# Modulation products queued in whole blocks, and recurrent states stored as transposed rows

## Chip, cores and metric

One core of a Trainium2 chip runs the whole kernel. The metric is device time in microseconds (us) of one execution, as the median of several.

## The reference, cut to what matters

Two layers of a trunk run for 128 context tokens and 512 latent tokens together. What the change touches is the modulation vector of each layer and the final state of the recurrence:

```python
for l in range(DEPTH):                                   # DEPTH = 2, D_MODEL = 1024
    mod_ctx = (jax.nn.silu(c_ctx) @ ada_w[l] + ada_b[l])[None, None, :]   # 6 * 1024 values
    y_p, (st, nk, nv, dk, dv) = trunk_layer(y_p, mod_ctx, context_mixer, p)
    mod_lat = (jax.nn.silu(c) @ ada_w[l] + ada_b[l])[:, None, :]
    y_s, _ = trunk_layer(y_s, mod_lat, latent_mixer, p)
...
sh_a, sc_a, g_a, sh_f, sc_f, g_f = jnp.split(mod, 6, axis=-1)   # shift, scale, gate of both halves of a layer
...
hf = linear_scan(af, bf, h0f, False); hb = linear_scan(ab, bb, h0b, True)
return y, hf[:, -1], hb[:, 0]        # st: 2 directions x 512 values per layer, an output of the kernel
```

## The kernel before, in words

Both token groups are kept as 640 columns, with the features on the partitions. A layer is a mixer (recurrence, neighbourhood attention, differential attention, out projection) and a feed-forward network. Large products split each operand into a high and a low part and do three products for one (L265 to L267, L274 to L276, L1235 to L1237). Loads, TensorE products, splits on ScalarE (L110) and VectorE (L117), and everything else are written as one program; a scheduler orders each engine's instructions by priority, where an instruction written earlier goes first as soon as its inputs stand. The helper `later(n)` shifts that priority by n for what is written inside it.

**Modulation.** A group of 2048 of the 6144 modulation values is one generator `ada_group`. It takes eight steps. A step loads 1 MB of `ada_w` into a raw tile (L195, tile `adaw`) and issues four products (L204, tile `ada`), one for each 32-row strip of the accumulator, all with the same 32-column stationary operand `cT[:, k]` and 512 columns of weights each. Five such groups run (40 steps, 160 products, each of which shows as two records in the trace): two in the mixer of each layer and one, for layer 1, in the feed-forward network of layer 0. Who calls the generator advances it with `next(ada)` after a part of its own work, so a step stands between other products. Nothing ties a step's four products together: the scheduler may put others between them. The first 1024-column pieces of layer 0 are done ahead in `ada_first` in the same manner with 128 columns each.

**Raw tiles.** The pool `rawp` has two tiles. Weights of the in projection (`w`), `ffn_up` (`up`) and `ada_w` share them, so a load waits until a tile's reader is done. All DMAs stand in one queue, SyncE's (SP), in order.

**States.** The scan of block j writes the last value of each direction into column `nstate[:, l, dr, j]` (L705): 128 features on the partitions. After the mixer the program stores them (L1456) with one DMA for each direction, 128 partitions by 4 columns, which goes to DRAM as 512 pieces of 4 bytes. Its inputs stand early, so the scheduler puts both stores of a layer into the SP queue in the middle of the neighbourhood attention.

Of the kernel before, what the change touches and what calls it, by code (L numbers as in the profile page):

```python
# [2 lines left out]

# [1 line left out]

# [12 lines left out]
P = 128  # L18
D = 1024
KD = D // P  # L20
# [48 lines left out]
def trunk_kernel(ctx: ExitStack, tc: tile.TileContext, A, O):  # L69
    nc = tc.nc  # L70
# [123 lines left out]
    def ada_load(l, g, k, w):  # L194
        nc.sync.dma_start(w, dram(A["ada_w"], (l * D + k * P) * 6144 + g * 2048, ((6144, P), (1, 2048))))  # L195
        return w

    def ada_group(l, g):
        acc = ps_a.tile([P, 512], F32, tag="ada", name="ada")
        for k in range(KD):  # L200
            w = ada_load(l, g, k, raw_tile("adaw"))
            with later(50 if l and g == 0 else 0):
                for q in range(4):
                    nc.tensor.matmul(acc[32 * q:32 * q + 32], cT[:, k], w[:, q * 512:q * 512 + 512],  # L204
                                     start=(k == 0), stop=(k == KD - 1))
            yield
        row = g_tile(512, name="adar")
        copy("a", row, acc)
        pt = s_tile()
        for u in range(4):  # L210
            nc.tensor.transpose(pt[:, u * P:u * P + P], row[:, u * P:u * P + P], ident)
        o = mod[l][:, g * 16:g * 16 + 16, :]
        for s in range(2):
            nc.vector.tensor_tensor(
                o[:, :, s].rearrange("p (g u) -> p u g", u=4),
                pt.rearrange("p (u g c) -> p u g c", u=4, g=4)[:, :, :, s],
                vec[l][:, V_ADAB + g * 16:V_ADAB + g * 16 + 16].rearrange("p (g u) -> p u g", u=4), op=OP.add)
        if g in (0, 2):
            ada_scale(l, g // 2, 0, KD)
# [8 lines left out]
    def ada_first(part, ws):  # L228
        acc = o_tile()
        pt = acc[:, P:2 * P]  # L230
        for k in range(KD):
            for q in range(4):
                gemv = nc.tensor.matmul(acc[32 * q:32 * q + 32, :P], cT[:, k],
                                        ws[k][part][:, q // 2, q % 2 * P:q % 2 * P + P],
                                        start=(k == 0), stop=(k == KD - 1))
        row = g_tile(P, name="adar")
        copy("a", row, acc[:, :P])
        nc.tensor.transpose(pt, row, ident)
        for v in range(2):
            at = v * 8 + part * 2  # L240
            nc.vector.tensor_tensor(mod[0][:, at:at + 2, :], pt.rearrange("p (v g c) -> p v g c", v=2, g=2)[:, v, :, 0:2],
                                    vec[0][:, V_ADAB + at:V_ADAB + at + 2, None].to_broadcast([P, 2, 2]), op=OP.add)
        ada_scale(0, 0, part * 2, part * 2 + 2)
        return gemv.ins

    @contextmanager
    def later(n):
# [928 lines left out]
    def ffn(xt, l, h, fp, ada, last, pre, keep, rows):  # L1176
# [265 lines left out]
                norm_half(xt, l + 1, 0, 3, hn)  # L1442
        return (None, None) if last else (hn, nxt)

    def chain(*gens):
        for g in gens:
            yield from g

    pre = units, raws[3], first, groups
    for l in range(DEPTH):  # L1450
        last = l + 1 == DEPTH
        ada = chain(ada_group(l, 1), ada_group(l, 2))
        with tc.tile_pool(name="mix", bufs=1) as mix:
            xt, h, pre, keep = mixer(xt, l, h, mix, ada, pre)
        for dr in range(2):
            nc.sync.dma_start(dram(O["st"], l * 1024 + dr * 512, ((1, P), (128, 4))), nstate[:, l, dr])  # L1456
        if not last:
            rows = lambda l=l: (vecs_a(l + 1), vecs_b(l + 1), vecs_c(l + 1), *vecs_d(l + 1))
        ada = iter(()) if last else ada_group(l + 1, 0)
        with tc.tile_pool(name="ffn", bufs=1) as fp:  # L1460
            h, pre = ffn(xt, l, h, fp, ada, last, pre, keep, None if last else rows)
# [29 lines left out]
```

## Time and profile before

| | us |
|---|---|
| median of three | 1659.25 (1658.79 to 1660.96) |
| the profiled execution | 1654.66 |
| its span (first to last instruction of the program) | 1652.5 |

In the profile, PE is a TensorE product, PEld its weight load, DVE is VectorE, ACT is ScalarE, POOL is GpSimd and SPq is the queue of DMA issues. An arrow `out<-in` gives the tiles; a bracket at a row's end is idle time of that engine ahead of the row and what ended it. The mean granted clock of TensorE over the span is 0.989 of full speed. Times in the trace are microseconds from the span's start: layer 0 has its neighbourhood attention from about 150 to 215, its feed-forward network from about 400 to 860; layer 1 has the attention from about 970 to 1030.

### The profile page before, as it was taken

Reading aid. Unit: us, or ns where it says so; the run is one execution under the profiler, and the core shown is the slowest. Engines: PE = TensorE matmul, PEld = TensorE weight load, DVE = VectorE, ACT = ScalarE, POOL = GpSimd, SP = SyncE. Lnnn points to the kernel's source line nnn. Section 1 sums busy time; section 2 is a strip of 40 time slices with the busy share of each in tenths; the row PEclk is TensorE's granted clock in tenths of the full one; section 3 lists DMA queues with packets and bytes.
Section 4 is the critical chain, followed back from the end, with each engine's and each line's share of the span. In section 5 each row is a group of like instructions: output and inputs, shape, how many; then the busy total and the mean of one; then the engine's idle time right before and its main releaser. Section 6 shows DMA issues by size and latency. Waiting matters only on the chain.

```text
span 1652.5 us, 28654 instructions
## 1 busy us (share of the span) xinstructions
PE 1604.7 (97%) x11181; PEld 1471.0 (89%) x11181; DVE 1326.2 (80%) x2883; ACT 919.5 (56%) x1689; POOL 110.4 (7%) x98
## 2 busy tenths in 40 slices
PE   7998999999999999999999989999999999999998
PEld 5876688799988899999998766887999999999998
DVE  5985648888988788888897757578789998888884
ACT  5874547755645444554458646477466554445441
POOL 0320200102000000000012202001020000000000
PEclk8999999999999999999999989999999999999999
DMA  9556530231344322223243554420312223322221
GB/s 321 178 201 191 128 129 20 103 103 36 125 131 125 112 77 77 77 85 98 77 151 117 189 147 106 144 76 28 102 41 82 84 80 97 93 77 77 71 71 64
DMA packets 210149, 177.30 MB, mean 107 GB/s; under 512 B 49670, under 2 KB 199390, under 8 KB 203870
## 3 DMA queue, kind: packets, MB, share of 16 engines
q1 hardware_dynamic: 210014, 175.48, 35.3%
q8 instruction: 88, 1.44, 0.4%
q14 instruction: 47, 0.39, 0.1%
HBM read 165.12 MB, written 10.34 MB: 106 GB/s over the span
## 4 chain that ended last, share of the span: by engine, by line
PE 81%; DVE 7%; DMA 4%; ACT 3%; issue 2%; SPq 1%; POOL 0%; ACTq 0%; DVEq 0%; POOLq 0%
PE m L274 6%; PE m L276 6%; PE m L275 6%; PE m L1236 5%; PE m L1235 5%; PE m L1237 5%; PE s L276 4%; PE s L275 4%; PE s L274 4%; PE m L265 3%; PE m L267 3%; PE m L266 3%; PE t L1237 3%; PE t L1236 3%; PE t L1235 3%; PE ada L204 2%
## 5 line engine op out<-in xcount | busy, mean ns | idle before, releaser
L117 DVE TENSOR_TENSOR wl<-up,wh 128x1024 fp32r<-128x1024 f32 x126 | 156.2, 1245 | 37.1 <-ACT wh L110 36.1
L1293 DVE SCALAR_TENSOR_TENSOR u<-raw,vec,u 128x127 f32<-128x127 f32 x352 | 175.4, 545 | 0.8 <-ACT u L1287 0.8
L110 ACT ACTIVATE wh<-up 128x1024 fp32r<-128x1024 f32 x126 | 132.1, 1052 | 74.8 <-PE t L1237 42.2
L265 PE MATMUL m<-wh,h 128*128 128x256 f32 x480 | 141.8, 296 | 0.0
L266 PE MATMUL m<-wl,h 128*128 128x256 f32 x480 | 139.7, 291 | 0.0
L267 PE MATMUL m<-wh,h 128*128 128x256 f32 x480 | 139.2, 290 | 0.0
L274 PE MATMUL m<-act,wh 128*128 128x320 f32 (+2 forms) x376 | 117.1, 312 | 0.0
L275 PE MATMUL m<-act,wl 128*128 128x320 f32 (+2 forms) x376 | 116.6, 310 | 0.0
L276 PE MATMUL m<-act,wh 128*128 128x320 f32 (+2 forms) x376 | 116.5, 310 | 0.0
L274 PE MATMUL s<-act,wh 128*128 128x320 f32 (+2 forms) x376 | 116.3, 310 | 0.0
L275 PE MATMUL s<-act,wl 128*128 128x320 f32 (+2 forms) x376 | 116.3, 309 | 0.0
L276 PE MATMUL s<-act,wh 128*128 128x320 f32 (+2 forms) x376 | 116.1, 309 | 0.0
L276 PE MATMUL m<-h,wh 128*128 128x320 f32 (+2 forms) x352 | 109.8, 314 | 2.9 <-DVE h L117 1.9
L265 PEld LDWEIGHTS m<-wh,h 128*128 128x128 f32 x480 | 92.8, 193 | 22.3 <-issue 20.1
L274 PE MATMUL m<-h,wh 128*128 128x320 f32 (+2 forms) x352 | 111.2, 317 | 0.1
L275 PE MATMUL m<-h,wl 128*128 128x320 f32 (+2 forms) x352 | 110.0, 313 | 0.0
L528 DVE SCALAR_TENSOR_TENSOR xt<-m,mod,xt 128x128 f32<-128x128 f32 (+3 forms) x236 | 95.9, 432 | 14.1 <-PE m L276 13.1
L110 ACT ACTIVATE raw<-m 128x320 f32<-128x320 f32 x126 | 54.5, 432 | 88.0 <-PE m L1237 74.6
L266 PEld LDWEIGHTS m<-wl,h 128*128 128x128 f32 x480 | 93.1, 194 | 4.1 <-issue 3.4
L267 PEld LDWEIGHTS m<-wh,h 128*128 128x128 f32 x480 | 92.6, 193 | 4.1 <-issue 3.9
L1235 PE MATMUL m<-h,wh 128*128 128x320 f32 x304 | 94.7, 311 | 0.0
L1236 PE MATMUL m<-h,wl 128*128 128x320 f32 x304 | 94.2, 310 | 0.4 <-DVE wl L117 0.4
(361 smaller groups left out, 5095.1 us busy)
## 6 DMA issues: line engine op xcount, KB each, us to landing
up<-in_ffn_up_dram SPq DMA_DIRECT2D x88, 512.0 KB
adaw<-in_ada_w_dram SPq DMA_DIRECT2D x40, 1024.0 KB
w<-in_w_in_dram SPq DMA_DIRECT2D x16, 1024.0 KB
rawd<-in_ffn_down_dram SPq DMA_DIRECT2D x24, 512.0 KB
pro<-in_ada_w_dram SPq DMA_DIRECT2D x30, 256.0 KB
w<-in_w_out_dram SPq DMA_DIRECT2D x8, 768.0 KB
rawd<-in_ffn_down_dram SPq DMA_DIRECT2D x16, 384.0 KB
xd<-xt SPq DMA_DIRECT2D x4, 1280.0 KB
```

Source lines behind the costliest of these rows:

```text
L110: return nc.scalar.activation(out, in_, AF.Copy)
L117: (eng or nc.vector).tensor_tensor(out, a, b, op=OP.subtract)
L265: nc.tensor.matmul(out, st[0], mv[0], start=(i == 0), stop=False)
L266: nc.tensor.matmul(out, st[0], mv[1], start=False, stop=False)
L267: nc.tensor.matmul(out, st[1], mv[0], start=False, stop=(i == n - 1))
L274: nc.tensor.matmul(out, a[0], b[0], start=(k == total[0]), stop=False)
L275: nc.tensor.matmul(out, a[1], b[0], start=False, stop=False)
L276: last = nc.tensor.matmul(out, a[0], b[1], start=False, stop=(k == total[-1]))
L1235: nc.tensor.matmul(ps, st[0], mv[0], start=first and k == 0, stop=False, skip_group_check=chk)
L1236: nc.tensor.matmul(ps, st[1], mv[0], start=False, stop=False, skip_group_check=chk)
L1237: nc.tensor.matmul(ps, st[0], mv[1], start=False, stop=last and k == 3, skip_group_check=chk)
L1293: nc.vector.scalar_tensor_tensor(u[:, oa:ob], r[:, oa + sft:ob + sft], w, u[:, oa:ob], op0=OP.mult, op1=OP.add)
```

## The change

A step's four products go through a new helper `gemv4`. The first keeps the priority that it had. The other three get a priority 2000 ahead and an order edge behind the first (`issue_after`), so that as soon as the first is placed nothing else goes between. `ada_group` and `ada_first` both call it. The two column stores of a layer become `state_out`: TensorE transposes the 128 by 8 states into a PSUM tile of the pool `s`, VectorE copies 8 rows of 128 values, and one DMA stores 8 runs of 512 bytes.

```diff
+    def gemv4(acc, k, w):
+        head = None
+        for q in range(4):
+            with later(-2000 if q else 0), (tc.issue_after(head) if q else nullcontext()):
+                head = nc.tensor.matmul(acc[32 * q:32 * q + 32], cT[:, k], w(q), start=(k == 0),
+                                        stop=(k == KD - 1)).ins
+        return head
+
     def ada_group(l, g):
         acc = ps_a.tile([P, 512], F32, tag="ada", name="ada")
         for k in range(KD):
             w = ada_load(l, g, k, raw_tile("adaw"))
             with later(50 if l and g == 0 else 0):
-                for q in range(4):
-                    nc.tensor.matmul(acc[32 * q:32 * q + 32], cT[:, k], w[:, q * 512:q * 512 + 512],
-                                     start=(k == 0), stop=(k == KD - 1))
+                gemv4(acc, k, lambda q: w[:, q * 512:q * 512 + 512])
...
         for k in range(KD):
-            for q in range(4):
-                gemv = nc.tensor.matmul(acc[32 * q:32 * q + 32, :P], cT[:, k],
-                                        ws[k][part][:, q // 2, q % 2 * P:q % 2 * P + P],
-                                        start=(k == 0), stop=(k == KD - 1))
+            gemv = gemv4(acc[:, :P], k, lambda q: ws[k][part][:, q // 2, q % 2 * P:q % 2 * P + P])
...
+    def state_out(l):
+        pt = s_tile()
+        nc.tensor.transpose(pt[:8, :P], nstate[:, l].rearrange("p d j -> p (d j)"), ident)
+        row = g_tile(P, name="so")
+        copy("v", row[:8], pt[:8, :P])
+        nc.sync.dma_start(dram(O["st"], l * 1024, ((P, 8), (1, P))), row[:8])
...
-        for dr in range(2):
-            nc.sync.dma_start(dram(O["st"], l * 1024 + dr * 512, ((1, P), (128, 4))), nstate[:, l, dr])
+        state_out(l)
```

The lines of the kernel shift by 2 to 9 (L204 becomes L202, L1237 becomes L1240, L946 becomes L949, L356 becomes L359, L965 becomes L968).

In the program before, the 40 steps stand on TensorE as 59 runs of modulation products with other work between; in the changed one as 40 runs of four. Nine of the 19 runs less are in the mixers (five in layer 0, four in layer 1), ten in the feed-forward network of layer 0. The first place is there, on TensorE (`tx` and `h` are the network's inputs, `wh` and `wl` its weights); before:

```order
L1237 MATMUL m<-tx_4743,wh 128x320
L1235 MATMUL m<-tx_4742,wh 128x320
L204 MATMUL ada<-adaw,cT 32x512
L1236 MATMUL m<-tx_4742,wl 128x320
L204 MATMUL ada<-adaw,cT 32x512
L1237 MATMUL m<-tx_4743,wh 128x320
L204 MATMUL ada<-adaw,cT 32x512
L1235 MATMUL m<-tx_4742,wh 128x320
L204 MATMUL ada<-adaw,cT 32x512
L1236 MATMUL m<-tx_4742,wl 128x320
```

The four products of one step stand here as four runs, with one product of the network between each two. The same place, on TensorE, in the changed kernel:

```order
L1240 MATMUL m<-tx_4746,wh 128x320
L1238 MATMUL m<-tx_4745,wh 128x320
L202 MATMUL ada<-adaw,cT 32x512 x4
L1239 MATMUL m<-tx_4745,wl 128x320
L1240 MATMUL m<-tx_4746,wh 128x320
L1238 MATMUL m<-tx_4745,wh 128x320
```

The three others moved up to the first, and nothing else moved at this place. The second place is TensorE in the neighbourhood attention of layer 0 (`naset` holds queries and keys, `s` the scores; `m` is the in projection); before:

```order
L946 MATMUL s<-naset 128x128
L267 MATMUL m<-wh,h_339 128x256
L204 MATMUL ada<-adaw,cT 32x512 x3
L946 MATMUL s<-naset 128x128
L204 MATMUL ada<-adaw,cT 32x512
L265 MATMUL m<-wh,h_338 128x256
```

A score product splits the step into three and one. The same place, on TensorE, in the changed kernel:

```order
L949 MATMUL s<-naset 128x128
L270 MATMUL m<-wh,h_339 128x256
L202 MATMUL ada<-adaw,cT 32x512 x4
L949 MATMUL s<-naset 128x128
L268 MATMUL m<-wh,h_338 128x256
```

The fourth product moved ahead of the score product. The third place is the SP queue just ahead of that, in layer 0 (`nvd` is a scratch copy of the values, `t2d` one of the bias); before:

```order
L971 DMA naset<-nvd_982 128x1x128 x2
L1456 DMA out_dram<-nstate 128x4x1
L195 DMA adaw<-in_ada_w_dram 128x2048 x2
L1456 DMA out_dram<-nstate 128x4x1
L356 DMA w<-in_w_in_dram 128x8x256
L965 DMA naset<-t2d_983 128x8x32 x3
```

The two loads for the next two modulation steps stand behind one state store, and the next weights behind the other. The same place of the SP queue in the changed kernel:

```order
L974 DMA naset<-nvd_982 128x1x128 x2
L195 DMA adaw<-in_ada_w_dram 128x2048 x2
L359 DMA w<-in_w_in_dram 128x8x256
L968 DMA naset<-t2d_983 128x8x32 x2
L195 DMA adaw<-in_ada_w_dram 128x2048
L968 DMA naset<-t2d_983 128x8x32
```

Both stores left this place; the one that replaces them stands at the start of the feed-forward network.

## Rows read from the trace of the kernel before

**Rows 1.** The page: busy time of the engines; the last chain's shares.

```profile
PE 1604.7 (97%) x11181; PEld 1471.0 (89%) x11181; DVE 1326.2 (80%) x2883; ACT 919.5 (56%) x1689; POOL 110.4 (7%) x98
...
PE 81%; DVE 7%; DMA 4%; ACT 3%; issue 2%; SPq 1%; POOL 0%; ACTq 0%; DVEq 0%; POOLq 0%
```

**Rows 2.** Chain that ended last, in time: start, length, link; both attentions.

```profile
137.41 7.82 DMA w<-in_w_in_dram
...
148.72 12.14 DMA adaw<-in_ada_w_dram
...
165.43 8.80 DMA w<-in_w_in_dram
...
968.35 11.65 DMA adaw<-in_ada_w_dram
```

**Rows 3.** Stretches: length; busy PE, PEld, DVE, ACT, POOL; clock; DMA share; GB/s.

```profile
138.00:143.00 5.00, 5.00 (x33) 2.66 (x31) 5.00 (x12) 3.51 (x11) 0.00 (x0) 1.00 0.78 242
149.00:157.00 8.00, 7.73 (x60) 6.33 (x58) 0.98 (x2) 1.32 (x3) 0.00 (x0) 1.00 0.75 38
...
162.00:165.00 3.00, 3.00 (x7) 0.68 (x4) 0.81 (x4) 0.46 (x2) 0.00 (x0) 0.50 0.22 50
...
967.00:977.00 10.00, 7.47 (x58) 6.18 (x51) 2.98 (x6) 3.50 (x6) 0.00 (x0) 0.95 0.67 36
```

**Rows 4.** The SP queue in time, both attentions: start, us, line, transfer, count.

```profile
143.09 0.34 SPq L195 DMA_DIRECT2D adaw<-in_ada_w_dram  x1
...
146.82 0.43 SPq L1456 DMA_DIRECT2D out_dram<-nstate  x1
...
963.79 1.95 SPq L1456 DMA_DIRECT2D out_dram<-nstate  x2
```

**Rows 5.** TensorE in time, layer 0: a step of four products, eight records.

```profile
148.78 0.28 PE L266 MATMUL m<-wl,h 128*128 128x256 f32 x1
148.90 0.28 PE L267 MATMUL m<-wh,h 128*128 128x256 f32 x1
149.11 1.06 PE L204 MATMUL ada<-adaw,cT 128*32 128x512 f32 x8
150.10 0.39 PE L265 MATMUL m<-wh,h 128*128 128x256 f32 x1
```

**Rows 6.** TensorE in time, layer 0 feed-forward: single products, two records each.

```profile
528.52 1.05 PE L204 MATMUL ada<-adaw,cT 128*32 128x512 f32 x2
...
529.84 1.05 PE L204 MATMUL ada<-adaw,cT 128*32 128x512 f32 x2
```

**Rows 7.** Stretches as in rows 3: feed-forward of layer 0 and of layer 1.

```profile
469.80:530.80 61.00, 61.00 (x385) 53.80 (x381) 52.40 (x112) 30.80 (x44) 0.00 (x0) 1.00 0.43 130
1269.30:1335.30 66.00, 66.00 (x451) 65.87 (x451) 64.70 (x114) 36.25 (x53) 0.00 (x0) 1.00 0.32 92
```

**Rows 8.** TensorE in time, layer 0 attention: the split step and what follows.

```profile
160.91 1.93 PE L204 MATMUL ada<-adaw,cT 128*32 128x512 f32 x6 [4.18 <-DMA adaw<-in_ada_w_dram]
...
163.48 1.92 PE L204 MATMUL ada<-adaw,cT 128*32 128x512 f32 x2
...
168.10 0.48 PE L946 MATMUL s<-naset 64*128 64x128 f32 x2
```

**Rows 9.** TensorE in time, the same place in layer 1.

```profile
980.04 1.93 PE L204 MATMUL ada<-adaw,cT 128*32 128x512 f32 x6 [5.57 <-DMA adaw<-in_ada_w_dram]
...
987.27 0.49 PE L946 MATMUL s<-naset 64*128 64x128 f32 x2
```

**Rows 10.** TensorE in time: products of the recurrence that wait for VectorE.

```profile
112.89 0.38 PE L266 MATMUL s<-xs,gh 128*128 128x256 f32 x1 [0.79 <-DVE xs L117]
...
937.51 0.39 PE L266 MATMUL s<-xs,gh 128*128 128x256 f32 x1 [1.86 <-DVE xs L117]
```

**Rows 11.** TensorE in time, layer 0 attention: a later wait, for ScalarE.

```profile
176.12 0.43 PE L951 MATMUL t<-pT,naset 128*64 128x128 f32 x2 [1.47 <-ACT pT L110]
```

**Rows 12.** TensorE in time, end of the layer 0 mixer: a wait for GpSimd.

```profile
390.19 0.41 PE L276 MATMUL s<-h,wh 128*128 128x320 f32 x1 [1.99 <-POOL h L117]
```

More of the change, by code (lines that the diff above doesn't have):

```diff
@@ L1 @@
 import math
-from contextlib import ExitStack, contextmanager
+from contextlib import ExitStack, contextmanager, nullcontext
 import numpy as np
@@ L243, in ada_first @@
         ada_scale(0, 0, part * 2, part * 2 + 2)
-        return gemv.ins
+        return gemv
     @contextmanager
```

## The prediction

> **What bounds the kernel now.** I read the page's busy times and the shares of the last chain first. TensorE is busy 97% of the span and holds 81% of the chain; transfers hold 4% [rows 1]. So a microsecond taken from TensorE's own list comes off the end nearly anywhere, unless a wait swallows it, and the few transfers on the chain must be looked at one by one. The chain in order of time names them: in each layer's attention one modulation load takes 12.14 and 11.65 us from issue to use, and in layer 0 a load of weights 8.80 us behind it [rows 2]. Next I took the engines stretch by stretch. While those modulation loads are under way the DMA engines are 75% and 67% busy but move 38 and 36 GB/s; a few microseconds before the first it is 242 GB/s at 78% [rows 3]. The SP queue shows what was issued just ahead: the state stores, at 146.82 in layer 0 and both at 963.79 in layer 1 [rows 4]. Last, TensorE in order of time shows what one modulation product costs [rows 5, 6] and what the two late loads do to it [rows 8, 9].
>
> **The change, part by part.**
>
> **Whole blocks.** A step of four products takes from the start of the ordinary product before it to the start of the one behind it 150.10 − 148.90 = 1.20 us [rows 5]. A lone product with one ordinary product behind it takes 529.84 − 528.52 = 1.32 us [rows 6]; an ordinary product of this size is 66.00 / 451 = 0.146 us [rows 7], so the lone product costs 1.17 us. One costs what four cost: the price is per run. The order has 59 runs before and 40 after, so 19 runs go. Two of them lie in the two late-load stretches, costed below. The other 17 give 17 × 1.17 = 19.9 us of TensorE time.
>
> What swallows some of it? In the recurrence a product waits 0.79 us in layer 0 and 1.86 us in layer 1 for a VectorE subtraction [rows 10]. One of the 17 runs stands a few microseconds ahead of each. VectorE's list there (scans, a norm) does not start from that run, so TensorE would arrive 1.17 us earlier and wait that much longer: I take off 2 × 1.17 = 2.3. In the feed-forward network, where ten of the 17 are, VectorE is the next engine. It is busy 52.40 of 61.00 us in three iterations with modulation, 17.5 each; TensorE takes 20.3 each and, with a split of one step into three or four runs undone, about 18 [rows 7]. Layer 1 without modulation runs four iterations in 66.00 us with VectorE 98% busy and TensorE without a gap [rows 7], so VectorE can be worked that hard and I take all ten. If it cannot, up to 10 × 1.17 = 11.7 is lost (a rival). The order also has one block in that network some ten products sooner than before, 10 × 0.146 = 1.5 us, while its load comes no sooner for certain: between 0 and 1.5, I take 0.5 off, nearer to zero because the copy that frees its raw tile moves up as well. Net of this part: 19.9 − 2.3 − 0.5 = 17.1 us.
>
> **State stores out of the attention.** Layer 0: TensorE idles 4.18 us to 160.91; both runs of the split step then take 1.9 us where a block takes 1.06, since the granted clock stands at 0.50 there, the lower of its two levels, 1.2 GHz, behind the idle stretch; the score product behind is reached at 168.10 [rows 3, 5, 8]. From the start of the wait at 160.91 − 4.18 = 156.73 that is 11.4 us. With the load in time the same list is: the block, 1.20 less the 0.39 of the product already running, 0.8; a pair of scores, about 0.5 [rows 8]; fifteen products at 0.12 [rows 5], 1.8; changes between shapes, 0.3; together 3.4. Gain 7.9 to 8.0, I take 7.9. Layer 1 in the same way: from 980.04 − 5.57 = 974.47 to 987.27 is 12.8 [rows 9], less 3.4 is 9.4. Is the load then in time? The load issued at 143.09 is used at 149.11 without a wait, so an undisturbed one needs at most 6.0 us [rows 4, 5]. Issued at 148.72 [rows 2] it would stand by 154.7, needed at 156.73 or, with two runs less ahead, at 154.4; issued at 968.35 by 974.4, needed at 974.47, or 1.2 sooner. What the bound leaves is 0.3 and 1.1 us of wait at worst. I count none, since 6.0 is a ceiling, and let the range carry both.
>
> Behind it in layer 0 the weights issued at 165.43 took 8.80 us, against 7.82 for the same kind of load at 137.41 [rows 2], and ScalarE, which waited for them, made TensorE wait 1.47 us at 176.12 [rows 11]. I take the difference of the two loads, 1.0; between 0 and 1.5.
>
> The price of a store is best read as what it does to the queue: 1024 pieces of 4 bytes in layer 1 and then 10 us at 36 GB/s [rows 3], or about 10 ns for a piece. The new store has 8 pieces a layer: 0.1 us, at the start of the feed-forward network. The Trainium skill, page DMA: Bandwidth & Descriptors, section Specifications, gives 512 B as the least transfer for full rate and says that below it the engine reads, modifies and writes. By that rule the new runs of exactly 512 B cost nothing extra, and the sum stays; that a queue behind slows down, as the row shows, the section does not say.
>
> **The transpose, the copy and the store.** Two transposes on TensorE, about 0.4 us each by the pair of scores at 168.10 [rows 8]. The order puts them directly ahead of products of the network that in layer 0 wait 1.99 us for GpSimd [rows 12]; that wait covers the transpose. Without cover: 0.8 for both. The VectorE copy is one small operation a layer, under 0.3 each; the store stands behind a load that is issued early. I take zero, bounds 0 and 1.4. The PSUM tile of the transpose is held until the copy; the next claim on it comes behind that copy in the order.
>
> **Orders that move without a purpose.** In both attentions the softmax work on VectorE and the products around it stand in another order. The number of products is the same. Bounds: some 3 us either way over both layers, about two waits like the 1.47 [rows 11]; I take zero, since the stretch shows few such waits.
>
> Sum: 17.1 + 7.9 + 9.4 + 1.0 = 35.4 us. The profiled execution takes 1654.66 us, 2.2 of it outside the span of 1652.5; it would take 1619.3. The median of the runs shown is 1659.25, 4.6 above the profiled one; I carry that difference over: 1659.25 − 35.4 = **1623.9**, said as 1624.
>
> **The rivals.**
>
> *The stores are not what slows the loads.* Then the two waits stay, and of the stretches only the two removed runs go, at half clock 1.9 each. Gain 17.1 + 3.8 = 21, time 1638. For it: 4-byte pieces are few bytes. Against: both slow stretches begin behind a state store, and a value gather at the same place of the queue goes with 242 GB/s [rows 3, 4]. Chance 0.07.
>
> *VectorE takes over in the feed-forward network.* 11.7 lost, time 1636. For it: 17.5 against 18 us an iteration is a thin margin. Against: layer 1 [rows 7]. Chance 0.08.
>
> *Slower: the attention comes apart.* The new order there leaves TensorE standing for softmax chains. The mechanism is one wait like the 1.47 us [rows 11] at each of the 32 sets of scores of both layers: 47 us, time 1624 + 47 = 1671. It decides from 25 of the 32 on. Against: now hardly any of them waits, and the order keeps other products between a set of scores and its use. Chance 0.03.
>
> *It does not do what it says*, that is, runs still split: the order shows 40 whole blocks, so no chance.
>
> **How the numbers follow.** Forecast 1624 with 0.82; the rivals 0.07, 0.08 and 0.03. The forecast's own width: 3 us for the moved orders, 1.4 for the transposes and copies, 1.4 for the two loads, 1 for the weights, 1 for the block that comes sooner, on the one side; on the other 3 for the orders and 2.3 if the recurrence's waits do not swallow what I took off, and a clock that falls less often. So 1616 to 1632; reaching to the second rival gives **1616 to 1637**, which leaves the first rival and the slower one out, and tails of the forecast, together under 0.2. A measurement of this kernel can tell about 0.2%, 3.3 us, from no change. All cases but the slower one are faster by more; for small mishaps that add up to no change I leave 0.01: faster 0.96, same 0.01, slower 0.03.
>
> **What would show it.** Right: 40 modulation runs of eight records, each near 1.06 us; no wait for a modulation load over 1 us in either attention, hundreds of GB/s where 38 and 36 stood, no fall of the clock there; the two loads on the chain near 6 us or gone from it; waits for the recurrence's VectorE subtraction about 1.2 us longer; the network's iterations in layer 0 some 2.3 to 3.5 us shorter where a step had been split. Wrong: slow loads at the same place without a store ahead (first rival); TensorE waiting for VectorE between 460 and 560 us (second); waits for softmax tiles all through the attentions (third).

## The result, and the profile after

The changed kernel takes 1620.89 us (median; 1618.03 to 1624.47) against 1659.02 for the kernel before on the same chip: ratio 0.977, interval 0.975 to 0.980. By the medians that is 38.1 us. In the profiled executions the span went from 1652.5 to 1616.9 us, 35.6 us less, where the prediction's sum was 35.4. Executions of one kernel lay 4 to 6 us apart, so the two gains don't contradict each other.

The page of the changed kernel, busy time and shares of the last chain, as [rows 1]:

```profile
PE 1575.7 (97%) x11183; PEld 1466.1 (91%) x11183; DVE 1327.0 (82%) x2885; ACT 921.0 (57%) x1689; POOL 112.4 (7%) x98
...
PE 86%; DVE 6%; DMA 3%; ACT 2%; issue 2%; SPq 1%; POOL 0%; ACTq 0%; DVEq 0%; POOLq 0%
```

TensorE's own work fell by 29.0 us. The costliest groups show how much of that are modulation products; first the group in the kernel before, then the same in the changed one (busy, mean ns, idle ahead):

```profile
L204 PE MATMUL ada<-adaw,cT 128*32 128x512 f32 x320 | 65.8, 627 | 10.4 <-DMA adaw<-in_ada_w_dram 10.3
```

```profile
L202 PE MATMUL ada<-adaw,cT 128*32 128x512 f32 x320 | 42.6, 605 | 1.9 <-DMA adaw<-in_ada_w_dram 1.9
```

The same 320 records are busy 23.2 us less, and the idle time for their loads is down from 10.4 to 1.9. Not all of the 23.2 is the price of runs: the two split steps behind the late loads ran at half clock, 3.85 us each in two runs [rows 8; layer 1 alike] where a block takes 1.06, so 5.6 us are theirs. The other 17 runs come to 17.6, or 1.04 each, the length of a lone product in [rows 6]. Where the two late loads stood, the stretches (columns as in [rows 3]), the SP queue and TensorE now read:

```profile
150.00:157.00 7.00, 7.00 (x59) 5.90 (x57) 0.69 (x1) 1.08 (x2) 0.00 (x0) 1.00 0.84 298
...
944.00:951.00 7.00, 7.00 (x54) 5.66 (x53) 1.65 (x4) 2.07 (x3) 0.00 (x0) 1.00 0.80 300
```

```profile
149.57 2.06 SPq L195 DMA_DIRECT2D adaw<-in_ada_w_dram  x2
...
943.83 0.80 SPq L195 DMA_DIRECT2D adaw<-in_ada_w_dram  x2
```

```profile
157.72 1.06 PE L202 MATMUL ada<-adaw,cT 128*32 128x512 f32 x8
...
948.81 1.06 PE L202 MATMUL ada<-adaw,cT 128*32 128x512 f32 x8
```

298 and 300 GB/s stand where 38 and 36 stood [rows 3]; TensorE is busy without a gap at full clock; the blocks start without a wait, where it was 4.18 and 5.57 us [rows 8, 9]. New are longer waits in the recurrence and one ahead of the attention (TensorE in order of time):

```profile
113.95 0.38 PE L269 MATMUL s<-xs,gh 128*128 128x256 f32 x1 [1.63 <-DVE xs L117]
...
144.43 0.27 PE L174 MATMUL s<-ident,vr 88*128 88x88 f32 x1 [1.52 <-issue]
...
914.51 0.39 PE L269 MATMUL s<-xs,gh 128*128 128x256 f32 x1 [2.72 <-DVE xs L117]
```

To see where the time went, each TensorE product was matched with the same product of the kernel before (line, tiles, order of occurrence), and the difference of their starts, called the lag here, read at the stages' ends. The table gives what each stage of the profiled execution gained (minus) or lost, beside the prediction's terms and two experiments (below). Stages are cut by times of the kernel before.

| stage (us of before) | predicted | changed | blocks only | rows only |
|---|---|---|---|---|
| start, 0 to 100 | 0 | +0.9 | −0.2 | −0.1 |
| recurrence, layer 0, to 150 | −2.3 | +0.2 | 0.0 | −0.1 |
| neighbourhood attention, to 230 | −10.1 | −11.9 | −0.6 | −9.0 |
| differential attention, out projection, to 400 | 0 | +0.4 | +2.4 | +0.9 |
| feed-forward, layer 0, to 560 | −11.2 | −12.5 | −11.6 | −0.8 |
| recurrence, layer 1, 860 to 950 | 0.0 | −1.6 | +0.2 | −1.6 |
| neighbourhood attention, to 1050 | −11.7 | −12.7 | −3.3 | −8.5 |
| differential attention, out projection, to 1200 | 0 | +1.5 | +1.5 | 0.0 |
| feed-forward, layer 1, to the end | 0 | +0.8 | −1.5 | −0.2 |

From 560 to 860 us nothing moved. The changed kernel's stages add up to 34.9 us; the remaining 0.7 lies behind the last product. A second profile of the same kernel (`e11_changed_again`, below) has the same −11.9 and −12.7 in the two neighbourhood attentions; its other stages differ from the column by 0.1 to 0.9, and by about 1.5 in two, recurrence and differential attention of layer 1, where the clock fell in one of the two executions only.

### The profile page after: what moved, and what is told of

Same layout as the page of the kernel before. It is cut to its first block, busy times and chain, and to the rows that moved or that the text cites. A ratio compares the mean times of both kernels' runs of the same rounds, so it can differ in the third digit from the quotient of the medians.

```text
span 1616.9 us, 28663 instructions
## 1 busy us (share of the span) xinstructions
PE 1575.7 (97%) x11183; PEld 1466.1 (91%) x11183; DVE 1327.0 (82%) x2885; ACT 921.0 (57%) x1689; POOL 112.4 (7%) x98
## 4 chain that ended last, share of the span: by engine, by line
PE 86%; DVE 6%; DMA 3%; ACT 2%; issue 2%; SPq 1%; POOL 0%; ACTq 0%; DVEq 0%; POOLq 0%
PE m L277 6%; PE m L279 6%; PE m L278 6%; PE m L1238 6%; PE m L1239 6%; PE m L1240 6%; PE s L278 4%; PE s L279 4%; PE s L277 4%; PE m L268 4%; PE m L270 4%; PE m L269 4%; PE t L1240 3%; PE t L1238 3%; PE t L1239 3%; PE t L934 2%
## 5 line engine op out<-in xcount | busy, mean ns | idle before, releaser
L117 DVE TENSOR_TENSOR wl<-up,wh 128x1024 fp32r<-128x1024 f32 x126 | 156.3, 1245 | 38.1 <-ACT wh L110 37.1
L268 PEld LDWEIGHTS m<-wh,h 128*128 128x128 f32 x480 | 91.8, 191 | 14.5 <-issue 11.2
L1240 PE MATMUL t<-tx,wh 128*128 128x320 f32 x304 | 94.2, 310 | 0.0
```

The source lines that it names most:

```text
L117: (eng or nc.vector).tensor_tensor(out, a, b, op=OP.subtract)
L268: nc.tensor.matmul(out, st[0], mv[0], start=(i == 0), stop=False)
L1240: nc.tensor.matmul(ps, st[0], mv[1], start=False, stop=last and k == 3, skip_group_check=chk)
```

## Experiments

**Each part alone.** `e1_blocks` is the changed kernel with the old stores put back; they stand in the SP queue exactly where they stood before. `e2_rows` is the kernel before with the new state store.

```diff
# e1_blocks, against the changed kernel
-        state_out(l)
+        for dr in range(2):
+            nc.sync.dma_start(dram(O["st"], l * 1024 + dr * 512, ((1, P), (128, 4))), nstate[:, l, dr])
# e2_rows, against the kernel before (with state_out as in the change)
-        for dr in range(2):
-            nc.sync.dma_start(dram(O["st"], l * 1024 + dr * 512, ((1, P), (128, 4))), nstate[:, l, dr])
+        state_out(l)
```

> The changed kernel with the two old column stores of each layer put back where they stood (512 pieces of 4 bytes each, ahead of the two modulation loads); the modulation blocks stay whole. Theory (two causes: 19 runs fewer, and column stores that slow the loads behind them): the two waits for a modulation load in the attentions come back, 4 to 7 us each, with the half clock behind them and loads of 10 us and more at some 40 GB/s. Of the 35.6 us by which the span got shorter, the two stretches hold 8.0 and 9.5; the two runs that went there keep 1.9 each at half clock, so 13.7 are lost again, and about 1.5 of the weights load in layer 0: gain left 20.4, time near 1639 (1638 to 1642, since a block that comes sooner waits longer for the same load). Rival (the stores don't slow the loads; the old waits came from the split blocks): as the changed kernel, 1621, no wait over 1 us.

> The kernel before with only the state store changed (transpose on TensorE, one store of 8 runs of 512 bytes); the modulation products stay split in 59 runs. Theory: both waits for a modulation load are gone, both loads land about 4 to 6 us after issue, no fall of the clock there; gain 7.9 + 9.4 + 1.0 less the two runs that stay, 1.2 each: 16, time near 1643 (1640 to 1646). Rival (the stores don't slow the loads): no gain, 1659, with the 4 and 5 us waits still there.

Measured: `e1_blocks` 1641.54 us, ratio 0.991 (0.988 to 0.993), span 1639.1; `e2_rows` 1635.58, ratio 0.987 (0.985 to 0.989), span 1632.4. Both are gains: 13.4 and 20.1 us of span. Stretches, and TensorE in order of time, of `e1_blocks`:

```profile
149.00:157.00 8.00, 7.51 (x58) 6.21 (x56) 0.98 (x2) 1.53 (x3) 0.00 (x0) 1.00 0.78 35
957.00:965.00 8.00, 6.71 (x54) 6.17 (x50) 2.74 (x6) 1.51 (x4) 0.00 (x0) 1.00 0.64 29
```

```profile
161.06 1.94 PE L202 MATMUL ada<-adaw,cT 128*32 128x512 f32 x8 [4.55 <-DMA adaw<-in_ada_w_dram]
...
970.50 1.93 PE L202 MATMUL ada<-adaw,cT 128*32 128x512 f32 x8 [6.80 <-DMA adaw<-in_ada_w_dram]
```

With the column stores back, 35 and 29 GB/s, the waits and the half clock (1.94 for a block) are back, though every block is whole. The waits are 0.4 and 1.2 us longer than in [rows 8, 9]: a run saved ahead of a load that comes no sooner is waited for instead. The stretches of `e2_rows` show the reverse, with the steps still split:

```profile
150.00:157.00 7.00, 7.00 (x57) 6.26 (x56) 0.98 (x2) 0.53 (x2) 0.00 (x0) 1.00 0.61 255
956.00:963.00 7.00, 7.00 (x58) 5.92 (x56) 2.26 (x4) 1.09 (x2) 0.00 (x0) 1.00 0.63 229
```

So the stores alone made the loads late, and the first rival falls. The time of `e1_blocks` lies in its expected range, but only because the kernel before took 1656.03 us on that chip: it gained 14.5 us by the medians, 13.4 of span, where 20.4 were expected. Against the changed kernel its two attentions lost 11.3 and 9.4 us, 20.7 together, where the expectation had 15.2; the runs saved there were waited for as well. Another 1.6 went into the differential attention of layer 0, where the clock fell (0.50 from 314 to 317 us). `e2_rows` gained 4 us more than expected: its two attentions gave 9.0 and 8.5 us, where the expectation had 7.9 + 1.0 − 1.2 = 7.7 and 9.4 − 1.2 = 8.2, and 1.6 more came in layer 1's recurrence, where the clock did not fall in this execution (last section). The two parts together, 33.5, are nearly the whole of the 35.6.

**Place or pieces.** `e3_late_columns` puts 4-byte stores at the place of the new store; `e4_early_rows` puts the new store at the old place.

```diff
# e3_late_columns, in state_out
-        copy("v", row[:8], pt[:8, :P])
-        nc.sync.dma_start(dram(O["st"], l * 1024, ((P, 8), (1, P))), row[:8])
+        cp = nc.vector.tensor_copy(row[:8], pt[:8, :P])
+        late = tiny.tile([P, 8], F32, tag="late", name="late", bufs=1)
+        with tc.issue_after(cp.ins):
+            nc.vector.tensor_copy(late, nstate[:, l].rearrange("p d j -> p (d j)"))
+        for dr in range(2):
+            nc.sync.dma_start(dram(O["st"], l * 1024 + dr * 512, ((1, P), (128, 4))), late[:, dr * 4:dr * 4 + 4])
# e4_early_rows, in the mixer; the call behind the mixer goes, and the row gets a tile of its own
+        state_out(l)
         with later(400):
             na_prompt()
...
-        row = g_tile(P, name="so")
+        row = tiny.tile([P, P], F32, tag="so", name="so", bufs=1)
```

> The changed kernel, but at the place of the new row store (start of the feed-forward network) stand the two old column stores, 1024 pieces of 4 bytes a layer, read from a copy that VectorE makes there; the transposes stay and their result is not stored. Theory (pieces cost what is queued right behind them, for some 10 us, and nothing else): the next load in the queue is issued about 16 us later in layer 0, so time as the changed kernel, 1621 (1619 to 1624). Rival (1024 small pieces cost the queue 10 us wherever they stand, and TensorE pays in the end): 1626 to 1641.

> The changed kernel with its row store (transposes, copy, one store of 8 runs of 512 bytes) moved up to the old place, directly ahead of the two modulation loads in layer 1 and of the value gather and these loads in layer 0. Theory (the number of pieces is what counts, not that a store stands there): loads behind it land 4 to 6 us after issue, no wait over 1 us; time as the changed kernel but for two transposes without cover, 1621 to 1624. Rival (any store there that has to wait or to write holds up the loads): the two waits come back, 1630 to 1639.

Measured: 1621.67 and 1621.55 us, both ratio 0.978 (0.976 to 0.980); spans 1619.4 and 1620.5. Both are as fast as the changed kernel. The SP queue of `e3_late_columns` behind the first stores, and that of `e4_early_rows` in layer 1:

```profile
393.30 0.94 SPq L1457 DMA_DIRECT2D out_dram<-late  x2
409.09 0.35 SPq L195 DMA_DIRECT2D adaw<-in_ada_w_dram  x1
```

```profile
945.84 0.32 SPq L1454 DMA_DIRECT2D out_dram<-so  x1
947.91 0.82 SPq L195 DMA_DIRECT2D adaw<-in_ada_w_dram  x2
```

1024 small pieces cost nothing where no load is issued for 15.8 us behind them (it is the same in layer 1); a store of 8 rows costs nothing two microseconds ahead of the loads. Either half of the store's change, the layout or the place, would have done.

**What a small piece costs.** Three kernels do nothing but trials: a store, right behind it two loads of 1 MB, then a VectorE operation that needs both. Its wait is the measure; each of the three kernels ran once. The stores of the first trial kernel; `columns(1, ...)` is one direction's column store:

```diff
+    def columns(n, st, k, eng=None):
+        for d in range(n):
+            to = scratch.tile([512], F32, name="kept")
+            (eng or nc.sync).dma_start(dram(to, 0, ((1, P), (P, 4))), st[:, 4 * (d % 2):4 * (d % 2) + 4])
+    def pieces(rows, per, size, st, k):
+        to = scratch.tile([rows * per, 2 * size], F32, name="kept")
+        nc.sync.dma_start(dram(to, 0, ((2 * size * per, rows), (2 * size, per), (1, size))),
+                          st[:rows, :per * size].rearrange("p (a b) -> p a b", a=per))
```

> Leaves the whole computation out: it only writes zeros to the outputs and then, one trial after the other, issues a store and right behind it two loads of 1 MB of the modulation weights, as in the attention. Trials: no store; 512, 1024 and 2048 pieces of 4 bytes; 8 pieces of 512 bytes; 128 of 32 bytes; 512 of 64 bytes; 512 of 512 bytes; 1024 pieces of 4 bytes from ScalarE's queue instead; 1024 pieces with the loads issued only when they have landed; 1024 pieces of 4 bytes read instead of written; no store. Theory (the price is per piece, about 10 ns): the two loads land in about 7 us without a store and with 8 pieces; 5, 10 and 20 us later behind 512, 1024 and 2048 pieces of 4 bytes; pieces of 32 and 64 bytes cost about as much each, 1.3 and 5 us; 512 of 512 bytes 1 to 2 us; behind landed stores nothing. Rival (the price is for bytes or per store, not per piece): all stores of 4 KB and less alike, within 1 us of no store.

VectorE in order of time in `e5_loads_behind`; the inputs name the trial, the bracket is its wait:

```profile
41.12 0.69 DVE L105 TENSOR_TENSOR stcolB<-colAx,colAy 128x512 f32<-128x512 f32 x1 [17.46 <-DMA colAy<-in_ada_w_dram]
59.38 0.69 DVE L105 TENSOR_TENSOR stcolD<-colBx,colBy 128x512 f32<-128x512 f32 x1 [17.32 <-DMA colBy<-in_ada_w_dram]
87.64 0.69 DVE L105 TENSOR_TENSOR strows<-colDx,colDy 128x512 f32<-128x512 f32 x1 [27.32 <-DMA colDy<-in_ada_w_dram]
96.21 0.69 DVE L105 TENSOR_TENSOR stpieA<-rowsx,rowsy 128x512 f32<-128x512 f32 x1 [7.64 <-DMA rowsy<-in_ada_w_dram]
...
114.31 0.69 DVE L105 TENSOR_TENSOR stpieC<-pieBx,pieBy 128x512 f32<-128x512 f32 x1 [8.37 <-DMA pieBy<-in_ada_w_dram]
...
142.23 0.69 DVE L105 TENSOR_TENSOR stcolW<-colQx,colQy 128x512 f32<-128x512 f32 x1 [17.64 <-DMA colQy<-in_ada_w_dram]
154.41 0.48 DVE L114 MEMSET stcolW<- 128x512 f32 x1 [11.24 <-DMA kept<-stcolW]
162.63 0.69 DVE L105 TENSOR_TENSOR stcolR<-colWx,colWy 128x512 f32<-128x512 f32 x1 [7.49 <-issue]
172.38 0.69 DVE L105 TENSOR_TENSOR stlast<-colRx,colRy 128x512 f32<-128x512 f32 x1 [8.73 <-DMA colRy<-in_ada_w_dram]
180.80 0.17 DVE L120 TENSOR_TENSOR stend<-lastx,lasty 128x8 f32<-128x8 f32 x1 [7.48 <-DMA lasty<-in_ada_w_dram]
```

Without a store the wait is 7.48 us in the last trial (7.39 and 7.45 in the two kernels below). The first trial has no store either and waited 16.62, but its loads were issued only at 12 us, behind the seven writes of zeros. Behind 512 pieces of 4 bytes (colA) it is 10.0 longer, behind 1024 (colB) 9.8, behind 2048 (colD) 19.8; behind 8 rows 0.2, behind 512 pieces of 64 bytes with as much space between them (pieB) 0.9. From another engine's queue (colQ) the price is the same. 1024 pieces take 11.24 us to land, and loads issued after that are as fast as any (colW, 7.49). Reads of 4 bytes (colR) cost 1.3. The effect is there and has the size seen in the kernel, but the theory's price per piece is wrong: 512 cost as much as 1024. The next kernel asks whether neighbours in DRAM matter.

> Leaves the whole computation out and writes zeros to the outputs, as the trials before it, with other stores ahead of the two loads of 1 MB. Measured so far: without a store VectorE waits 7.5 us for both loads; behind 512 or 1024 pieces of 4 bytes 17.3 to 17.6, behind 2048 it is 27.3, behind 512 pieces of 64 bytes, with 64 bytes between them, 8.4. The pieces of the column store are neighbours in DRAM that come from neighbouring partitions. Trials, 512 pieces each: 4 bytes close together; 4 bytes with 60 bytes between them; 4 bytes with 508 bytes between them; 8, 16, 32 and 64 bytes close together; then 128 and 256 pieces of 4 bytes close together; 512 of 4 bytes again; no store. Theory one (neighbours: pieces that lie next to each other in DRAM have to be worked off one after the other): with space between them, 4 bytes cost under 1.5 us, waits of 7.5 to 9; close together the cost falls as the piece grows, about 10, 5, 2.5 us for 4, 8, 16 bytes; 128 and 256 pieces cost 2.5 and 5. Theory two (size alone: every small piece costs about 19 ns wherever it lies): 4 bytes cost 10 us with or without space; 128 and 256 pieces 2.5 and 5.

```diff
+    def pieces(st, per, size, gap):
...
+        step = size + gap
+        to = scratch.tile([P * per * step], F32, name="kept")
+        nc.sync.dma_start(dram(to, 0, ((step, P), (P * step, per), (1, size))),
+                          st[:, :per * size].rearrange("p (a b) -> p a b", a=per))
```

VectorE in `e7_pieces`: 512 pieces of 4 bytes close together, the same with 60 bytes between them, 512 of 8 and of 16 bytes close together, 128 of 4 bytes:

```profile
40.11 0.69 DVE L97 TENSOR_TENSOR stlineA<-closex,closey 128x512 f32<-128x512 f32 x1 [17.13 <-DMA closey<-in_ada_w_dram]
49.53 0.69 DVE L97 TENSOR_TENSOR stlineB<-lineAx,lineAy 128x512 f32<-128x512 f32 x1 [8.48 <-DMA lineAy<-in_ada_w_dram]
...
70.95 0.69 DVE L97 TENSOR_TENSOR stfours<-pairsx,pairsy 128x512 f32<-128x512 f32 x1 [10.79 <-DMA pairsy<-in_ada_w_dram]
81.59 0.69 DVE L97 TENSOR_TENSOR steight<-foursx,foursy 128x512 f32<-128x512 f32 x1 [9.70 <-DMA foursy<-in_ada_w_dram]
...
116.17 0.69 DVE L97 TENSOR_TENSOR sttwice<-oncex,oncey 128x512 f32<-128x512 f32 x1 [15.82 <-DMA oncey<-in_ada_w_dram]
```

With space between them the same 512 pieces cost 1 us (8.75 with 508 bytes of space). Close together, 8, 16, 32 and 64 bytes wait 10.79, 9.70, 8.01 and 7.93. So neighbours are what costs, not smallness. But 128 neighbours cost 8 us already, where the theory gave 2.5, and 256 cost as much as 512 (a wait of 17.30), where it gave 5.

> Leaves the whole computation out and writes zeros to the outputs; trials as before with single values of 4 bytes only, one from each partition, ahead of the two loads of 1 MB. Measured so far: no store 7.4 to 7.5 us of wait, 128 neighbouring pieces 15.8, 512 neighbouring 17.2, 512 with 60 bytes between them 8.5. Trials: 16, 32, 64 and 128 neighbours; 128 with 4, 12 and 28 bytes between them; 128 in groups of 16 neighbours and of 4 neighbours, the groups 512 bytes apart. Theory one (pieces in the same 64 bytes are worked off one after the other, about 0.5 us each, and different 64 bytes side by side): 16, 32, 64 and 128 neighbours all about 15; gaps of 4, 12 and 28 bytes 11.5, 9.5 and 8.5; groups of 16 about 15, of 4 about 9.5. Theory two (pieces in the same 512 bytes one after the other, 60 ns each): 16, 32, 64 neighbours 8.5, 9.5, 11.5; gaps 11.5, 9.5, 8.5; groups of 16 about 8.5, of 4 about 8.

```diff
+    def run(st, n, gap=0, group=None):
...
+        to = scratch.tile([n * P], F32, name="kept")
+        dims = ((128, n // group), (1, group)) if group else ((1 + gap, n),)
+        src = st[:n, :1]
+        nc.sync.dma_start(dram(to, 0, (*dims, (1, 1))), src)
```

VectorE in `e8_runs`, 16, 32 and 64 neighbouring pieces of 4 bytes:

```profile
33.10 0.69 DVE L96 TENSOR_TENSOR stthirty<-sixteenx,sixteeny 128x512 f32<-128x512 f32 x1 [9.41 <-DMA sixteeny<-in_ada_w_dram]
46.19 0.69 DVE L96 TENSOR_TENSOR stsixty<-thirtyx,thirtyy 128x512 f32<-128x512 f32 x1 [12.14 <-DMA thirtyy<-in_ada_w_dram]
61.87 0.69 DVE L96 TENSOR_TENSOR stall<-sixtyx,sixtyy 128x512 f32<-128x512 f32 x1 [14.74 <-DMA sixtyy<-in_ada_w_dram]
```

128 neighbours wait 15.41; gaps of 4, 12 and 28 bytes 10.59, 9.28 and 8.52; groups of 16 and of 4 neighbours 10.29 and 9.28. Theory one (15 us for all the first four) falls; theory two has the order right and the size wrong: up to 64 neighbours the price is 0.11 to 0.15 us for each, and further ones hardly add. How wide the region is in which they get in each other's way, and what in the memory does it, stays open.

The Trainium skill, page DMA: Bandwidth & Descriptors, section Specifications, says that transfers under 512 B are read, modified and written. That may be what neighbours do to each other here, but no run shows it; the runs do show that size alone isn't the price, since 512 pieces of 64 bytes, or of 4 bytes with space between them, cost 0.5 to 1.4 us.

**Why one product costs what four cost.** `e6_one_strip` sends all four products of a step into the same strip; the other strips are filled with zeros.

```diff
+    def gemv1(acc, k, w):
...
+                head = nc.tensor.matmul(acc[:32], cT[:, k], w(q), start=(k == 0 and q == 0),
+                                        stop=(k == KD - 1 and q == 3)).ins
...
+        nc.vector.memset(acc[32:64], 0.0)
+        nc.vector.memset(acc[64:], 0.0)
...
-                gemv4(acc, k, lambda q: w[:, q * 512:q * 512 + 512])
+                gemv1(acc, k, lambda q: w[:, q * 512:q * 512 + 512])
```

> The changed kernel with the four products of a modulation step of the 40 steps all into the first 32-row strip of the accumulator, still queued as one run; the modulation values come out wrong by that. Theory (a run costs one product's time because its four products lie on four strips and run at once; a lone product leaves three strips empty): a step takes about four times as long, 4 x 0.9 = 3.5 to 4.2 us instead of 1.06, and the kernel 40 x 2.6 = some 100 us more, less what waits swallow: 1700 to 1730. Rival (a run costs an entry into and an exit from the odd shape, and the products in it are nearly free): a step 1.1 to 1.3 us, the kernel 1621 to 1631.

Measured: 1726.1 us (one run), some 105 more than the changed kernel took on another chip. A step in TensorE's order of time, and the group (columns as above):

```profile
80.05 3.62 PE L210 MATMUL ada<-adaw,cT 128*32 128x512 f32 x8
```

```profile
L210 PE MATMUL ada<-adaw,cT 128*32 128x512 f32 x320 | 146.1, 600 | 3.0 <-DMA adaw<-in_ada_w_dram 3.0
```

3.62 us against 1.06: on four strips the four products run at once, on one strip one after the other. So a run's price is not an entry fee but the streaming of 512 columns, once for up to four strips. The rival falls. The Trainium skill, page TensorEngine Tiling (Array Packing), section When to Use Tiling, names four-fold column tiling for a 32-wide stationary operand; the trace agrees with 3.4-fold.

**The runs in the mixers.** `e9_copied_out` frees the tile that TensorE waits for at 144 us: a ScalarE copy takes the modulation values out of PSUM, and VectorE adds the bias from SBUF. `e10_network_blocks` queues the steps as blocks only in the feed-forward network (`ada_first` keeps `gemv4`); `e11_changed_again` is the changed kernel beside it.

```diff
# e9_copied_out, in ada_group
+        ps, pt = pt, g_tile(512, name="adat")
+        copy("a", pt, ps)
# e10_network_blocks
-                gemv4(acc, k, lambda q: w[:, q * 512:q * 512 + 512])
+                if l and g == 0:
+                    gemv4(acc, k, lambda q: w[:, q * 512:q * 512 + 512])
+                else:
+                    for q in range(4):
+                        nc.tensor.matmul(acc[32 * q:32 * q + 32], cT[:, k], w[:, q * 512:q * 512 + 512],
+                                         start=(k == 0), stop=(k == KD - 1))
```

> The changed kernel with one ScalarE copy more in each of the five modulation groups: the transposed modulation values go from the PSUM tile into SBUF, and VectorE adds the bias from there. It answers where the three runs less in the recurrence of layer 0 went: there TensorE now stands 1.52 us for a PSUM tile whose reader, an addition on VectorE, is queued behind some 8 us of scans. Theory (the tile is what it waits for): the wait is gone, the rest of layer 0 comes about 1.3 us sooner, time 1619.5 against 1621. Rival (the next work waits for VectorE's scans anyway): the 1.5 us turn up again within 30 us, 1621 to 1622.

> The changed kernel, but only the eight steps in the feed-forward network are queued as blocks; in the mixers the four products of a step stand as before, nine runs more (49 in all). Theory (a run less is worth its 1.17 us only where TensorE is the bound; in the mixers the time goes to waits for VectorE and for loads): the kernel with only the state store changed had a span of 1632.4; less 10 x 1.17 = 11.7 is 1620.7, only 3.8 us more than the changed kernel's 1616.9, and the recurrence of layer 0 no later at its end. Rival (every run is worth 1.17 us, as the sum had it for seven of the nine): 1616.9 + 9 x 1.17 = 1627.4, 10.5 us more.

> The changed kernel itself, on the same chip beside the run above. Every theory expects about 0.977 of the kernel before; the difference of the two ratios is what the nine runs in the mixers are worth: 3.8 us (0.23%) by the first theory, 10.5 us (0.63%) by the second.

`e9_copied_out`: ratio 0.976 (0.974 to 0.979), 1618.51 us, not to be told from the changed kernel. The 1.52 us wait is gone, yet the products behind it stand where they stood to 0.3 us: from 118 us on, ahead of the place, they are 1.3 us later. The clock took that. Behind the wait for `xs` at 114 us, which is as long in both kernels (1.63 and 1.64), it fell in this execution and not in that of the changed kernel. The stretch (columns as in [rows 3]), in the changed kernel and then in `e9_copied_out`:

```profile
114.00:118.00 4.00, 4.00 (x28) 3.70 (x29) 0.00 (x0) 2.72 (x6) 0.61 (x1) 1.00 0.06 16
```

```profile
114.00:118.00 4.00, 4.00 (x19) 3.78 (x18) 0.00 (x0) 1.53 (x3) 0.00 (x0) 0.58 0.03 9
```

From 1.3 us later to 0.2 sooner is 1.5 us, the size of the wait, and the products stay 0.2 sooner to the end of the attention: in the trace the tile is what TensorE waited for, and the rival falls. The times can't tell 1.3 us, so they don't show this to be a better version. `e10_network_blocks`: 1625.42 us, ratio 0.981 (0.979 to 0.983), against 1620.47, 0.978 (0.977 to 0.980), for the changed kernel on the same chip. The difference is 0.24%, 4.0 us (5.0 by the medians), with intervals that overlap; the spans, 1626.2 and 1617.9, differ by 8.3, but 2.5 of that is a stretch at half clock in the differential attention of layer 0 (0.51 from 306 to 312 us). That leaves 5.8. The first theory (3.8) is nearer than the rival (10.5), but neither is hit; the prediction's sum had 8.3 for the nine, 5.9 and 1.2 for each of the two in the late stretches. In the recurrence of layer 0, `e10_network_blocks` is at its end as early as the changed kernel (+0.2 us over the stage against +0.2 and +0.6 in its two profiles): three runs less bought nothing there. Nor did the one run in layer 1's recurrence (−0.1 us over the stage in both kernels on this chip). It is the attentions that differ: 9.1 and 8.8 us gained there, against 11.9 and 12.7 in the changed kernel. So the nine runs are of two kinds. The five in the attentions are worth 6.7 us, somewhat more than five times 1.17; the four in the recurrences nothing. Both theories had treated them alike.

## Why the prediction was right, point by point

**Whole blocks in the network: right.** Ten runs, 11.7 predicted; the same stage gained 12.5, 11.6 and 12.5 us in the changed kernel, `e1_blocks` and `e10_network_blocks`, and 11.6 in `e11_changed_again`. The half microsecond for a block that comes sooner does not show as lost. VectorE did not take over: one stretch of the changed kernel, nearly the whole of the network's part with modulation, shows TensorE without a gap.

```profile
390.00:547.00 157.00, 156.97 (x1065) 147.55 (x1064) 144.71 (x287) 90.10 (x143) 0.00 (x0) 1.00 0.40 124
```

**Whole blocks in the recurrence: mis-sized.** I took off 1.17 for each of the two waits for `xs`. They grew by 0.84 (0.79 to 1.63) and 0.86 (1.86 to 2.72), so that much was right. But layer 0 had further waits that before were covered by the split runs: 0.37 for the cached keys at 135 us, and the 1.52 at 144, where a PSUM tile's reader on VectorE stands behind some 8 us of scans (the row names no releaser; `e9_copied_out`, where the wait is gone, shows it). All of the 3.5 us of three runs was swallowed, not a third of it. The step that failed is the 1.17 taken off for one wait in layer 0: TensorE meets VectorE's queue and a late load at two more places there, and waits at each.

**State stores: right.** 7.9 and 9.4 predicted for the two stretches; the lag of the products around them moves by 8.0 (between 156 and 166 us) and 9.5 (between 974 and 986). The list with the load in time thus took 3.4 and 3.3 us, as added up, though the 0.3 in it for changes between shapes stood on no row. The weights behind (1.0, bound 1.5) gave 1.5: the wait of [rows 11] is gone. The loads were in time, at 300 GB/s: in layer 1 the one issued at 943.83 is used at 948.81 without a wait, 5.0 us later, so 6.0 was a ceiling indeed. What spoke against the first rival was read loosely: the 242 GB/s are those of a weights load issued behind a value gather, and [rows 4] do not show the gather. The price of "about 10 ns for a piece" was wrong as a rule (512 and 1024 neighbours cost the same 10 us, 512 with space about 1), and harmless, as 8 rows cost 0.2.

**Transposes, copy, store: right.** The two transposes take 0.27 us each; the wait for GpSimd that should cover the first is 1.88 instead of 1.99 [rows 12]. The stages around lost 0.4 and, in layer 1's network, 0.8.

**Moved orders: within the bounds.** The attentions gained another 1.2 and 0.9 us beyond the terms, inside the 3 either way; the third rival's waits for softmax tiles did not appear.

**Not foreseen.** A fall of the clock in layer 1's differential attention took 1.5 us back in this profile. The stage table's misses (+2.5 in layer 0's recurrence, −1.8 and −1.0 in the neighbourhood attentions, −1.3 in the network, −1.6 for a clock that did not fall in layer 1's recurrence, +1.5 for one that did later, +2.1 in the remaining stages) cancel to 0.5 us, so part of the exact hit is luck; the large terms (7.9, 9.4 and 11.7) were each within 1 us. The median came out 3.0 us below the forecast of 1623.9, and 2.8 of that is the distance between profiled execution and median that the forecast carried over: 4.6 before, 1.8 (1619.05 to 1620.89) in the changed kernel.

## What to carry to other kernels

Products that share the array side by side cost as one only if nothing comes between them, so count runs, not products, and expect the full price of a run back only where TensorE itself is the bound: here in the network and in the attentions once their loads came in time, not in the recurrences. A store that scatters 4-byte neighbours from many partitions into one stretch of DRAM delayed the loads issued right behind it by some 10 us, and the row to find is the slow load, not the store: transpose it into rows, or put it where no load follows soon (15.8 us were enough here). A microsecond saved ahead of another engine's queue is waited for there.

## Of the hardware, not expected

The clock does not follow from the work of a stretch alone. In layer 1's recurrence TensorE stood for VectorE in both kernels, 1.86 us before and 2.72 after. The stretch, in the kernel before and then in the changed one (columns as in [rows 3]):

```profile
936.00:938.00 2.00, 0.49 (x3) 0.49 (x4) 2.00 (x4) 0.12 (x1) 0.00 (x0) 1.00 0.00 0
938.00:940.00 2.00, 2.00 (x13) 2.00 (x12) 0.95 (x2) 1.95 (x4) 0.00 (x0) 0.64 0.31 66
```

```profile
913.00:915.00 2.00, 0.49 (x3) 0.49 (x4) 2.00 (x4) 0.00 (x0) 0.00 (x0) 1.00 0.00 0
915.00:917.00 2.00, 2.00 (x17) 2.00 (x16) 0.95 (x2) 1.95 (x4) 0.00 (x0) 1.00 0.31 66
```

Behind the same 0.49 us of work in 2 us the clock fell once and once it did not, though the wait was longer. In `e11_changed_again`, the changed kernel once more, it fell at this place too, behind a wait of 2.74 us:

```profile
915.50:917.50 2.00, 1.85 (x7) 1.86 (x8) 1.56 (x3) 0.85 (x2) 0.00 (x0) 0.52 0.30 64
```

The same kernel in two profiled executions, the same three small waits in layer 1's differential attention, and the same busy time of TensorE; first the changed kernel, then `e11_changed_again`:

```profile
1092.50:1094.50 2.00, 0.74 (x4) 0.51 (x4) 2.00 (x7) 1.99 (x3) 1.60 (x2) 1.00 0.00 0
1094.50:1096.50 2.00, 1.91 (x7) 1.89 (x8) 2.00 (x10) 1.02 (x4) 0.00 (x0) 0.51 0.00 0
```

```profile
1095.10:1097.10 2.00, 0.74 (x4) 0.51 (x4) 2.00 (x5) 1.99 (x3) 1.65 (x2) 1.00 0.00 0
1097.10:1099.10 2.00, 1.85 (x13) 1.86 (x14) 2.00 (x11) 1.08 (x4) 0.00 (x0) 1.00 0.00 0
```

Behind the same 0.74 us of work in 2 us the granted clock fell to 0.51 once and stayed at 1.00 once; that is 1.5 us. It fell there in `e1_blocks`, `e3_late_columns` and `e10_network_blocks` too, and not in `e2_rows`, `e4_early_rows`, `e9_copied_out` or the kernel before. What decides it stays open; differences of this size between single profiles are not to be explained by the edit. The other surprise is the neighbours: 64 values of 4 bytes, 256 bytes in all, hold up 2 MB of loads by 7 us.
